# Pooling's joining gate as a stage of seven products, and the last addition of each attention result on GpSimd

## The chip, the core and the metric

The kernel runs on one core of one Trainium2 chip. The metric is the device time of one execution in microseconds, here the median of three runs. A core has TensorE (PE in the profile; PEld are its weight loads), VectorE (DVE), ScalarE (ACT), GpSimd (POOL) and SyncE (SP), which only issues DMAs here. Each engine works through its own list of instructions in order and waits on semaphores for the others.

## The reference, cut to what matters

One decoder block with two parallel branches, on 1024 positions of 1024 channels, in float32:

```python
proj = h @ w_in                       # h: the normalised, modulated input
q, k, v, z_a, u, z_b, m_a, m_b = jnp.split(proj, offs, axis=-1)   # 8 x 1024 columns
attn = stick_breaking_attention(to_heads(q), to_heads(k), to_heads(v))   # 16 heads of 64
p_a = (attn * jax.nn.silu(z_a)) @ w_branch_a
pooled = multiscale_causal_pool(u, pool_w, pool_scale)
p_b = (pooled * jax.nn.silu(z_b)) @ w_branch_b
merged = jax.nn.sigmoid(m_a) * p_a + jax.nn.sigmoid(m_b) * p_b
out = merged @ w_out
return x + gate[:, None, :] * out     # then a final RMS norm
```

The two joining gates are sigmoid(m_a) for attention and sigmoid(m_b) for pooling. In stick-breaking attention a weight is the sigmoid of its own logit times the product of (1 - sigmoid) of all keys between it and the query; the kernel forms that product with a scan along the keys.

## The kernel before

Every matrix is split into a high and a low part, and a product of two matrices is three passes: high by high, high by low, low by high. The input h is kept transposed in `hT`, both parts, 8 blocks of 128 channels by 1024 positions. A column tile is 128 columns of `w_in`; its product with h is 8 blocks x 3 passes for each half of the positions, so 2 x 24 matmuls of 128x128 by 512.

**Stages, in order.** First the modulation, the normalisation and `u` (tiles `ua`, `u`). Then the values, by `seven` (line 565), which multiplies two matrices of 1024x1024, each seen as 2x2 quarters, with seven products of quarters instead of eight (p1, p5, p6, p7, p4, p3, p2; each 2 halves x 4 columns of blocks x 6 matmuls = 48). The sums of quarters of h are made once beforehand (`make_t`, tiles `ht`); those of the weights are made on the way by VectorE, and `copied` and `added` (ScalarE, VectorE) join the products. `values` then splits each result and stores it to DRAM (`v_d`). Then pooling's own gate and projection (`wzb`), and the branch's matrix, again by `seven` (`bp`). The eight banks of PSUM go by four tags of two banks; `any_bank` takes them in turn, and `seven` is told which pair of tags its first chain takes.

**The attention** takes the heads in 8 pairs. For a pair there are three column tiles, keys, queries and gate `za` (`CK`, `CQ`, `CZA`), and in between stand the column tiles of the two joining gates (`CMA`, `CMB`), whose sigmoids go to DRAM. All these tiles are filler: `projections` (line 824) yields after each block of 3 matmuls, a quantum, and `step` (line 1008) weaves so many quanta between the attention's own instructions. `GATES` says how many gate tiles stand in each pair, `QUANTA` how many quanta a pair uses up (70); 37 and 25 quanta go ahead of the first pair, and what is left (18) comes after the last.

A pair has eight units (head h, quarter t of the queries), in `HT_ORDER`. For a unit, `z_items` (line 888) makes logits row block by row block: two matmuls into a bank `z`, two sigmoids on ScalarE (`om` = 1 - sigmoid, `be` = sigmoid), masks on the diagonal block by two selects on GpSimd (line 912), the scan of `om` on VectorE (line 914) and the multiplication of `be` by it. This is done three units ahead. `turn` (line 919) transposes weights chunk by chunk on TensorE into a bank `wt` (two banks), which ScalarE copies (high part) and VectorE subtracts (low part, line 934); two chunks are turned ahead of `product`, so the transposes of the chunk after next wait for a chunk's subtraction. `finish` (line 950) takes the unit's result, which lies in PSUM as three parts: a copy (line 958), two additions on VectorE (line 960), and once both heads are there, the multiplication by `za` on GpSimd and the store to DRAM (lines 963 and 964). A row of logits has up to 1024 keys for t = 0 and as few as 128 for t = 3. The junction of two pairs is where the t = 0 rows of the next pair (1024 and 896 keys) are scanned while its first unit asks for its four chunks.

The weights of each column tile are loaded by SyncE, copied by ScalarE and subtracted by GpSimd (line 116). SyncE's queue also holds the moves of keys and queries between partitions (line 785) and the stores of results. Matmuls, transposes and some others stand in the order of the program; the rest is ordered by the scheduler.

**The final stage** multiplies the gated attention by `w_branch_a` (`pa`), joins the branches with the two gates, read back from DRAM (`sa_d`, `sb_d`), and multiplies by `w_out` (`o`).

Of the kernel before, what the change touches and what calls it, by code (L numbers as in the profile page):

```python
# [21 lines left out]
QUANTA = (70,) * 8  # L22

GATES = (0, 1, 2, 1, 2, 1, 1, 2)
# [27 lines left out]
def block_kernel(ctx, tc, a, out):  # L52
# [17 lines left out]
    turns = [cycle(("av", "tr", "pj", "z")), cycle(("pj", "z", "av", "tr"))]  # L70
# [63 lines left out]
    gates = [c + j for j in range(KB) for c in (CMA, CMB)]  # L134
# [430 lines left out]
    def seven(nm, sums, load, b_of, a_moves, ta, tb, final):  # L565
# [36 lines left out]
        for name in ("p1", "p5", "p6", "p7", "p4", "p3", "p2"):  # L602
# [15 lines left out]
            for j in range(4):  # L618
# [4 lines left out]
                elif name == "p7":  # L623
                    final(1, 1, j, added(copied("s3", 4, j, ps[j]), chain["b"][j]))
                elif name == "p4":
                    final(1, 0, j, ps[j] if a_moves else copied("s3", 4, j + 4, ps[j]))
                elif name == "p3":
                    final(0, 1, j, added(keep["s2", j], ps[j]))
                elif name == "p2":
                    final(0, 0, j, added(keep["s1", j], ps[j]))  # L630

    with pool("vp") as vp:
# [34 lines left out]

        with pool("vs", side="right") as vs:
# [3 lines left out]

            def h_parts(name, q):
                if name in ("p1", "p2", "p3"):
                    k, n = dict(p1=(0, 0), p2=(1, 0), p3=(1, 1))[name]
                    return lambda m, e: hT[:, m, 4 * k + 2 * q + e, 512 * n:512 * n + 512]
                return b_op(k2(tq[("p5", "p6", "p7", "p4").index(name)], q), vs, 2, f"v{name}b{q}")
# [12 lines left out]
            seven("v", vs, load_v_w, h_parts, True, ("av", "tr"), ("pj", "z"), values)  # L690

    turns.pop(0)
# [61 lines left out]
    seven("b", sums, load_b_w, g_parts, False, ("pj", "z"), ("av", "tr"), branch)  # L754
# [5 lines left out]
    with pool("at") as at:  # L760
# [63 lines left out]
        def projections():  # L824

            todo = []
            gates = [(c + j, j, d_) for j in range(KB) for c, d_ in ((CMA, sa_d), (CMB, sb_d))]
# [13 lines left out]
            for i, (ct, p, use) in enumerate(todo):  # L841
# [6 lines left out]
                if gate:  # L848
                    out_ = sigmoid_out(at, 3, use[p], f"m{ct}")
# [100 lines left out]
        def finish(u):  # L950
# [4 lines left out]
            if h == 0:  # L955
                both[t] = at.tile([P, 256], F32, tag="tp", bufs=3, name=f"tp{p}_{t}")
            tp = both[t]
            act.copy(tp[r], av[64:128, 0])
            for i in range(2):
                v.tensor_add(tp[r], av[0:64, i], tp[r])  # L960
            if h == 1:
                sl = slice(t * 256, t * 256 + 256)
                gp.tensor_mul(tp, tp, pair[p]["za"][:, sl])
# [228 lines left out]
```

## Time and profile before

| what | value |
|---|---|
| median of three runs | 1191.57 us (1191.53 to 1192.69) |
| the profiled execution | 1194.0 us, its span 1192.3 us |
| TensorE busy | 1179.2 us (99%) |
| VectorE, ScalarE, GpSimd busy | 826.6, 542.3, 255.1 us |
| values (`vp`) | from 128.3 to 204.5 us |
| pooling's gate (`wzb`), branch (`bp`) | to 291.5, to 368.9 us |
| attention with its filler | to 1011.1 us |
| one pair in the middle | 73.1 us |

A row of the groups reads: line, engine, operation, output<-inputs by the program's names, shapes, count, busy time and mean length of one in ns, then the engine's idle time just before them and who ended it. A row of the timeline reads: start, length, engine, line, operation, tiles, shapes, count, and in brackets the idle time ahead with its releaser. A matmul's length is longer than its share of TensorE, since matmuls are pipelined; the distance from start to start counts. Line numbers are those of the kernel before.

### The profile page before, as it was taken

The numbers are of one execution on the slowest core, as the hardware profiler recorded it, in microseconds if no ns is written. First come the engines' busy times: TensorE is split into PE (matmuls) and PEld (weight loads), VectorE is DVE, ScalarE is ACT, GpSimd is POOL, SyncE is SP. The second block draws the span as 40 slices with busy tenths as digits, with TensorE's granted clock in tenths as the row PEclk, the third lists the DMA queues.
The fourth block names the chain that finished last, engine by engine and source line by source line (L and its number), as shares of the span: only waits on it lengthen the run. The fifth ranks groups of instructions, "written<-read, shape, count | busy, mean of one in ns | idle before, by whom it ended". The sixth has DMA issues, their size and how long they took to land.

```text
span 1192.3 us, 15804 instructions
## 1 busy us (share of the span) xinstructions
PE 1179.2 (99%) x5650; PEld 984.6 (83%) x5650; DVE 826.6 (69%) x1093; ACT 542.3 (45%) x1016; POOL 255.1 (21%) x384
## 2 busy tenths in 40 slices
PE   8999999999999999999999999999999999999997
PEld 7888888888888788888888888888888888888886
DVE  5767466698762577877778687786877853885643
ACT  5561354322541555556556565555555643232111
POOL 1000000000003233244333344333434431000001
PEclk9999999999999999999999999999999999999999
DMA  9652329653457331422415224152321224974612
GB/s 349 259 187 98 131 91 318 229 192 89 142 175 237 92 98 46 136 84 89 106 47 137 85 85 100 56 137 76 113 78 58 71 102 177 346 267 160 228 54 88
DMA packets 73312, 167.26 MB, mean 140 GB/s; under 512 B 9233, under 2 KB 22673, under 8 KB 71058
## 3 DMA queue, kind: packets, MB, share of 16 engines
q1 hardware_dynamic: 65026, 151.38, 39.2%
q10 hardware_dynamic: 8208, 14.88, 3.4%
q8 instruction: 44, 0.72, 0.3%
q14 instruction: 34, 0.28, 0.1%
HBM read 115.89 MB, written 33.56 MB: 125 GB/s over the span
## 4 chain that ended last, share of the span: by engine, by line
PE 82%; DVE 7%; DMA 5%; issue 4%; POOL 1%; ACT 1%; SPq 1%; POOLq 0%; ACTq 0%; DVEq 0%
PE p L101 33%; PE pa L101 7%; PE o L101 6%; PE vp L101 6%; PE z L101 5%; PE av L101 5%; PE wt L101 5%; PE u L101 5%; PE bp L101 4%; PE ua L101 3%; DMA u<-u_d 2%; PE wm L101 1%; DVE om L914 1%; DMA kh<-kh 1%; DVE gb L716 1%
## 5 line engine op out<-in xcount | busy, mean ns | idle before, releaser
L101 PE MATMUL p<-hT,w 128*128 128x512 f32 x1920 | 479.9, 391 | 0.0
L101 PEld LDWEIGHTS p<-hT,w 128*128 128x128 f32 x1920 | 355.2, 188 | 73.9 <-DVE klo L101 0.2
L914 DVE TENSOR_TENSOR_SCAN om<-om 128x512 f32<-128x512 f32 (+7 forms) x128 | 191.2, 1494 | 85.0 <-ACT om L907 51.9
L116 POOL TENSOR_TENSOR w<-w_raw,w 128x1024 fp32r<-128x1024 f32 x39 | 97.2, 2491 | 414.7 <-ACT w L121 409.7
L907 ACT ACTIVATE om<-z 128x512 f32<-128x512 f32 (+2 forms) x192 | 94.6, 493 | 157.1 <-PE z L101 134.6
L934 DVE TENSOR_TENSOR wt<-wt,wt 128x512 fp32r<-128x512 f32 (+1 forms) x160 | 99.4, 621 | 39.4 <-ACT wt L933 38.7
L912 POOL TENSOR_SCALAR_AFFINE_SELECT om<-om 128x128 f32<-128x128 f32 x128 | 72.7, 568 | 205.2 <-ACT om L907 201.8
L933 ACT CAST wt<-wt 128x512 fp32r<-128x512 f32 (+1 forms) x160 | 88.0, 550 | 49.4 <-PE wt L101 49.0
L101 PE MATMUL av<-wt,vv 128*128 128x512 f32 x320 | 106.3, 413 | 0.0
L101 DVE TENSOR_TENSOR be<-be,om 128x511 f32<-128x511 f32 (+7 forms) x128 | 101.1, 794 | 2.0 <-POOL be L912 0.7
L908 ACT ACTIVATE be<-z 128x512 f32<-128x512 f32 (+2 forms) x192 | 94.0, 490 | 0.0
L101 PE MATMUL wt<-ident,be 128*128 128x128 f32 x576 | 89.8, 273 | 1.8 <-DVE wt L934 1.8
L101 PE MATMUL pa<-ga,wa 128*128 128x512 f32 x384 | 89.6, 389 | 0.1
L101 PE MATMUL o<-wo,mhl 128*128 128x512 f32 (+1 forms) x408 | 89.6, 377 | 0.0
L101 PE MATMUL wzb<-hT,wzb 128*128 128x512 f32 x384 | 87.2, 389 | 0.0
L101 PEld LDWEIGHTS o<-wo,mhl 128*128 128x128 f32 x408 | 73.5, 188 | 14.1
L101 PEld LDWEIGHTS pa<-ga,wa 128*128 128x128 f32 x384 | 72.0, 188 | 15.4 <-DVE wa L116 0.5
L101 PEld LDWEIGHTS wzb<-hT,wzb 128*128 128x128 f32 x384 | 72.1, 188 | 14.9
L101 PEld LDWEIGHTS wt<-ident,be 128*128 128x128 f32 x576 | 69.8, 140 | 15.0 <-DVE wt L934 2.5
L101 PE MATMUL z<-kl,q 128*128 128x512 f32 (+2 forms) x192 | 65.5, 341 | 0.0
L101 PE MATMUL z<-kh,q 128*128 128x512 f32 (+2 forms) x192 | 64.0, 334 | 1.1 <-DMA q<-qlo 1.1
L101 PE MATMUL u<-hT,wg 128*128 128x512 f32 x240 | 55.5, 391 | 0.0
(217 smaller groups left out, 1482.0 us busy)
## 6 DMA issues: line engine op xcount, KB each, us to landing
w_raw<-in_w_in SPq DMA_DIRECT2D x40, 512.0 KB, 3.5
v_d<-vo SPq DMA_DIRECT2D x16, 512.0 KB, 4.1
vv<-v_d SPq DMA_DIRECT2D x8, 1024.0 KB, 5.6
wa_raw<-in_w_branch_a SPq DMA_DIRECT2D x16, 512.0 KB, 4.3
wa<-in_w_mod SPq DMA_DIRECT2D x7, 1024.0 KB, 7.5
kh<-kh SPq DMA_DIRECT2D x48, 128.0 KB, 2.3
va<-in_w_v SPq DMA_DIRECT2D x10, 512.0 KB, 3.6
ba<-in_w_branch_b SPq DMA_DIRECT2D x10, 512.0 KB, 4.2
```

The costliest lines, as they stand in the source:

```text
L101: ins = op(*args, **kw)
L116: lo_eng.tensor_tensor(lo, src, hi.bitcast(F32), op=ALU.subtract)
L716: v.scalar_tensor_tensor(z, dhls[j][:, sh * 512:sh * 512 + 512], psc_v[:, j:j + 1], z, ALU.mult, ALU.mult)
L907: act.activation(om[:, b0:b0 + n], zp[:, :n], AF.Sigmoid, scale=-0.125)
L908: act.activation(be[:, b0:b0 + n], zp[:, :n], AF.Sigmoid, scale=0.125)
L912: gp.affine_select(out=tl[:, :P], in_=tl[:, :P], pattern=[[1, P]], compare_op=ALU.is_gt, fill=fill, base=0, channel_multiplier=-1)
L914: v.tensor_tensor_scan(om[:, :W], om[:, :W], om[:, :W], 1.0, ALU.mult, ALU.min)
L933: act.copy(wt[:, 0, :off], pt[:, :off])
L934: v.tensor_sub(wt[:, 1, :off], pt[:, :off], wt[:, 0, :off].bitcast(F32))
```

## The change

Three things are changed together.

**Pooling's joining gate** (`CMB`) leaves the filler and becomes a third use of `seven`, directly behind the values. It reads the same sums of h (`h_parts` is made a function of the pool and the name). `gate_b` takes the sigmoid of each result on ScalarE (of p4's straight from PSUM, of the others from the joined copy) and stores it by SyncE. The weights `w_mb` come in the layout of `w_v`. `seven` gets a parameter `direct`, which says that p4's result is used where it lies in PSUM; the values had that before, and the branch doesn't get it. The tags of banks are exchanged for the new stage and the branch.

**The filler** then holds attention's gate only: 8 gate tiles instead of 16, one each in every other pair and four at the end, and a pair uses up 55 quanta instead of 70. Ten quanta are left after the last pair.

**In `finish`** ScalarE copies two of the three parts (`tl`, `tp`), VectorE adds the third to one of them, and GpSimd adds the two when both heads are there, just ahead of its multiplication.

```diff
-QUANTA = (70,) * 8
-GATES = (0, 1, 2, 1, 2, 1, 1, 2)
+QUANTA = (55,) * 8
+GATES = (0, 1, 0, 1, 0, 1, 0, 1)
...
-    gates = [c + j for j in range(KB) for c in (CMA, CMB)]
+    gates = [CMA + j for j in range(KB)]
...
-                    final(1, 0, j, ps[j] if a_moves else copied("s3", 4, j + 4, ps[j]))
+                    final(1, 0, j, ps[j] if direct else copied("s3", 4, j + 4, ps[j]))
...
+        with pool("ms", side="right") as ms:
+            def load_m_w(t, m, k, q):
+                nc.sync.dma_start(t.rearrange("p k c -> p (k c)"), a["w_mb"][m, 2 * k + q])
+            def gate_b(m, n, j, src):
+                t = ms.tile([P, 512], F32, tag="go", bufs=3, name=f"sb{4 * m + j}_{n}")
+                act.activation(t, src, AF.Sigmoid)
+                nc.sync.dma_start(sb_d[4 * m + j][:, 512 * n:512 * n + 512], t)
+            seven("m", ms, load_m_w, h_parts("m", ms), False, ("pj", "z"), ("av", "tr"), gate_b, True)
...
-    seven("b", sums, load_b_w, g_parts, False, ("pj", "z"), ("av", "tr"), branch)
+    seven("b", sums, load_b_w, g_parts, False, ("av", "tr"), ("pj", "z"), branch, False)
...
-                both[t] = at.tile([P, 256], F32, tag="tp", bufs=3, name=f"tp{p}_{t}")
-            tp = both[t]
-            act.copy(tp[r], av[64:128, 0])
-            for i in range(2):
-                v.tensor_add(tp[r], av[0:64, i], tp[r])
+                both[t] = [at.tile([P, 256], F32, tag=tag, bufs=3, name=f"{tag}{p}_{t}") for tag in ("tp", "tq")]
+            tp, tl = both[t]
+            act.copy(tl[r], av[64:128, 0])
+            act.copy(tp[r], av[0:64, 0])
+            v.tensor_add(tp[r], av[0:64, 1], tp[r])
             if h == 1:
                 sl = slice(t * 256, t * 256 + 256)
+                gp.tensor_add(tp, tp, tl)
                 gp.tensor_mul(tp, tp, pair[p]["za"][:, sl])
```

Three places show what moves. On GpSimd, at the junction of the second and third pairs, stood before (`om`, `be`: the selects, by head, row block; `w_13`: a weights' low part; `tp_1`: the result of t = 1):

```order
L912 AFFINE_SELECT om_0_5_4626<-om_0_5_4626 128x128
L912 AFFINE_SELECT be_0_5_4627<-be_0_5_4627 128x128
L116 TENSOR_TENSOR w_13_4663<-w_13_raw,w_13_4663 128x1024
L963 TENSOR_TENSOR tp_1_4469<-tp_1_4469,za_3626 128x256
L912 AFFINE_SELECT om_1_0_4671<-om_1_0_4671 128x128
L912 AFFINE_SELECT be_1_0_4672<-be_1_0_4672 128x128
```

and at the same junction of GpSimd's list stands now:

```order
L926 AFFINE_SELECT om_0_5_5086<-om_0_5_5086 128x128
L926 AFFINE_SELECT be_0_5_5087<-be_0_5_5087 128x128
L977 TENSOR_TENSOR tp_1_4942<-tp_1_4942,tq_1_4943 128x256
L978 TENSOR_TENSOR tp_1_4942<-tp_1_4942,za_4248 128x256
L926 AFFINE_SELECT om_1_0_5123<-om_1_0_5123 128x128
L926 AFFINE_SELECT be_1_0_5124<-be_1_0_5124 128x128
```

The added addition (L977) stands ahead of the select of the 1024-key row; the weights' low part, whose tile falls elsewhere now, does not. Of the seven junctions it stands directly ahead of that select at one now (the sixth) and at one before (this one).

On TensorE, behind the same junction, stood before (`av`: the products with the values; `p`: filler; `wt`: transposes; `z`: logits):

```order
L101 MATMUL av_0_0_4767<-wt_0_0_1_4716,vv_4504 128x512 x2
L101 MATMUL p_1_4744<-hT,w_12_4501 128x512 x6
L101 MATMUL wt_0_2_2_4805<-ident,be_0_4_4574 128x128 x2
L101 MATMUL wt_0_2_2_4805<-ident,be_0_5_4627 128x128
L101 MATMUL av_0_0_4767<-wt_0_0_2_4756,vv_4504 128x512 x2
L101 MATMUL p_1_4744<-hT,w_12_4501 128x512 x6
L101 MATMUL z_1_5_0_4823<-kh_3796,q_2_3968 128x384
```

and there stands now:

```order
L101 MATMUL av_0_0_5214<-wt_0_0_1_5166,vv_4895 128x512 x2
L101 MATMUL p_1_5186<-hT,w_10_4892 128x512 x6
L101 MATMUL wt_0_2_2_5249<-ident,be_0_4_5032 128x128 x2
L101 MATMUL wt_0_2_2_5249<-ident,be_0_5_5087 128x128
L101 MATMUL av_0_0_5214<-wt_0_0_2_5210,vv_4895 128x512 x2
L101 MATMUL p_1_5186<-hT,w_10_4892 128x512 x3
L101 MATMUL z_1_5_0_5264<-kh_4428,q_2_4669 128x384
```

The attention's own rows are the same; the filler between them is thinner. From the logits of the 1024-key row (`z_1_0_1`) to the transposes `wt_0_2_3` it is 39 matmuls before and 30 now.

On SyncE, at the end of the values, stood before (`v_d`: stores of values; `wzb_raw`: weights of the next stage; `u`: the next stage's input):

```order
L685 DMA v_d<-vo_0_1628 128x4x256
L685 DMA v_d<-vo_0_1633 128x4x256
L129 DMA wzb_raw<-in_w_in 128x1024
L685 DMA v_d<-vo_0_1638 128x4x256
L685 DMA v_d<-vo_0_1643 128x4x256
L703 DMA gbias<-in_b_gate 128x8
L526 DMA u_1662<-u_d 128x1024
```

and there stands now (`ma`: quarters of the new stage's weights):

```order
L687 DMA v_d<-vo_0_1628 128x4x256
L687 DMA v_d<-vo_0_1633 128x4x256
L697 DMA ma_1_1764<-in_w_mb 128x1024
L687 DMA v_d<-vo_0_1638 128x4x256
L687 DMA v_d<-vo_0_1643 128x4x256
L697 DMA ma_0_1728<-in_w_mb 128x1024
L697 DMA ma11s_1731<-in_w_mb 128x1024
L697 DMA ma_1_1766<-in_w_mb 128x1024
```

The stores of values stand where they stood. The new stage's first quarters come between them, and the quarters that its second product adds (`ma_0_1728`, `ma11s_1731` and the next) come behind the last store. In ScalarE's list at the end of the attention, the first weights of the final stage (`wa_0`) are now cast ahead of the last result read back (`ga_7`), and were cast behind it.

More of the change, by code (lines that the diff above doesn't have):

```diff
@@ L68, in bank @@
         return psp.tile([P, 512], F32, tag=tag, bufs=BANKS[tag], name=name)
-    turns = [cycle(("av", "tr", "pj", "z")), cycle(("pj", "z", "av", "tr"))]
+    turns = [cycle(("av", "tr", "pj", "z"))]
     def any_bank(name):
@@ L563, in added, with seven @@
         return t
-    def seven(nm, sums, load, b_of, a_moves, ta, tb, final):
+    def seven(nm, sums, load, b_of, a_moves, ta, tb, final, direct):
         s2k = sums.tile([P, 4, 512], F32, name=nm + "s2k")
@@ L666, in block_kernel, with h_parts, of @@
         early.close()
+        def h_parts(nm, pl):
+            def of(name, q):
+                if name in ("p1", "p2", "p3"):
+                    k, n = dict(p1=(0, 0), p2=(1, 0), p3=(1, 1))[name]
+                    return lambda m, e: hT[:, m, 4 * k + 2 * q + e, 512 * n:512 * n + 512]
+                return b_op(k2(tq[("p5", "p6", "p7", "p4").index(name)], q), pl, 2, f"{nm}{name}b{q}")
+            return of
         with pool("vs", side="right") as vs:
@@ L671, in load_v_w @@
                 nc.sync.dma_start(t.rearrange("p k c -> p (k c)"), a["w_v"][m, 2 * k + q])
[L673 to L677, printed above, removed]
             def values(m, n, j, src):
@@ L688, in values @@
                 )
-            seven("v", vs, load_v_w, h_parts, True, ("av", "tr"), ("pj", "z"), values)
-    turns.pop(0)
+            seven("v", vs, load_v_w, h_parts("v", vs), True, ("av", "tr"), ("pj", "z"), values, True)
+        with pool("ms", side="right") as ms:
[6 more added lines that the diff above has]
+            seven("m", ms, load_m_w, h_parts("m", ms), False, ("pj", "z"), ("av", "tr"), gate_b, True)
+    turns[0] = cycle(("av", "tr", "pj", "z"))
     diffs = ExitStack()
@@ L826, in projections @@
             todo = []
-            gates = [(c + j, j, d_) for j in range(KB) for c, d_ in ((CMA, sa_d), (CMB, sb_d))]
+            gates = [(CMA + j, j, sa_d) for j in range(KB)]
             for p in range(NP):
@@ L848, in projections @@
                 if gate:
-                    out_ = sigmoid_out(at, 3, use[p], f"m{ct}")
+                    out_ = sigmoid_out(at, 2, use[p], f"m{ct}")
                 for sh in range(2):
@@ L1159 @@
     w_v = np.asarray(w_in)[0][:, 2 * D:3 * D].reshape(4, 2, P, 2, 512).transpose(3, 0, 2, 1, 4)
+    w_mb = np.asarray(w_in)[0][:, CMB * P:CMB * P + D].reshape(4, 2, P, 2, 512).transpose(3, 0, 2, 1, 4)
     w_ut = np.asarray(w_in)[0][:, CU * P:CU * P + D].reshape(2, 512, 4, 2, P).transpose(2, 0, 4, 3, 1)
@@ L1178 @@
         "w_v": np.ascontiguousarray(w_v).reshape(2, 4, P, D),
+        "w_mb": np.ascontiguousarray(w_mb).reshape(2, 4, P, D),
         "pool_w": np.ascontiguousarray(np.asarray(pool_w)[0]),
```

## The prediction

> **What bounds the kernel now.** I read the page first, then the list of waits, then the timeline of TensorE alone, then the table of busy time by stage, and last the timeline of one junction between two pairs of heads.
>
> The page's first part and TensorE's own waits:
>
> ```profile
> PE 1179.2 (99%) x5650; PEld 984.6 (83%) x5650; DVE 826.6 (69%) x1093; ACT 542.3 (45%) x1016; POOL 255.1 (21%) x384
> ...
> PE wt L101 <- DVE wt L934: 1.8, 4, 0.5
> ...
> PE z L101 <- DMA q<-qlo: 1.1, 1, 1.1
> ```
>
> TensorE is busy 99% of the span and waits for other engines 3 us in the whole middle of the kernel. A busy TensorE can still hide waits, so the timeline of its groups decides (start, length, group, count):
>
> ```profile
> 128.32 11.04 PE L101 MATMUL vp<-vp1a,hT 128*128 128x512 f32 x48
> 139.20 11.04 PE L101 MATMUL vp<-vp5a,vp5b 128*128 128x512 f32 x48
> ...
> 204.48 87.20 PE L101 MATMUL wzb<-hT,wzb 128*128 128x512 f32 x384
> 291.52 11.17 PE L101 MATMUL bp<-p1b,bp1a 128*128 128x512 f32 x48
> ...
> 313.51 11.55 PE L101 MATMUL bp<-p6b,bp6a 128*128 128x512 f32 x48
> 324.90 11.15 PE L101 MATMUL bp<-p7b,bp7a 128*128 128x512 f32 x48
> ```
>
> From start to start, the values' seven products take 204.48 - 128.32 = 76.16 us for 336 matmuls, and the next stage 291.52 - 204.48 = 87.04 us for 384: 0.2267 us each in both, so nothing waits there. One product of the branch stage (its sixth) takes 324.90 - 313.51 = 11.39 us where 48 x 0.2267 = 10.88: about 0.4 us lost. So the time falls by 0.2267 us for each matmul taken away, until another engine is late. How near the others are, by stage (values; one turn of the loop over pairs):
>
> ```profile
> core 0: us, PE busy (x) PEld busy (x) DVE busy (x) ACT busy (x) POOL busy (x), PEclk, DMA share, GB/s
> 128.30:204.50 76.20, 76.20 (x338) 63.10 (x337) 49.35 (x53) 36.27 (x48) 0.00 (x0) 1.00 0.58 188
> 563.50:636.60 73.10, 73.10 (x373) 61.66 (x372) 57.22 (x76) 41.14 (x89) 25.26 (x40) 1.00 0.35 94
> ```
>
> A pair takes 73.1 us with TensorE at work in all of it; VectorE is busy for 57.22 of them (78%), and all clocks are at 1.00.
>
> **The change: matmuls.** Pooling's joining gate is 8 column tiles of 2 x 24 matmuls, 384, all of them filler in the attention; as seven products it is 7 x 48 = 336. The difference is 48 x 0.2267 = **10.9 us less**. This is the only gain. It takes 15 quanta of 3 matmuls from each of eight pairs: 45 x 0.2267 = 10.2 us, 73.1 becomes 62.9.
>
> **The new stage.** It has the matmuls of the values' stage, whose VectorE and ScalarE work (49.35 and 36.27 of 76.20 us) lay wholly beside TensorE. In place of 16 copies and 16 subtractions it has 16 sigmoids; I cost that at nothing, the cover being TensorE's 76.2 us. What is new is its entry: SyncE issues the weights of its second product behind the last stores of values. The end of the values, on SyncE, and the prices of what follows a load:
>
> ```profile
> 207.72 2.22 SPq L685 DMA_DIRECT2D v_d<-vo  x2
> ...
> va<-in_w_v SPq DMA_DIRECT2D x10, 512.0 KB, 3.6
> ...
> u<-u_d SPq DMA_DIRECT2D x8, 512.0 KB, 5.2
> ...
> L576 DVE TENSOR_TENSOR va<-va,va 128x1024 f32<-128x1024 f32 x2 | 2.4, 1218 | 0.0
> ...
> L548 ACT CAST vp5a<-va 128x1024 fp32r<-128x1024 f32 x2 | 2.1, 1051 | 0.0
> ```
>
> The stores are issued until 209.94, which is 5.5 us after the values' last matmul (204.48). Issue 0.35 (estimated from such rows) and landing 3.6 make 9.4; the addition 1.22 and the cast 1.05 make 11.7. The second product is due at 10.88: **0.9 us** lost, my value, since a load of the same kind and size takes 3.6. The ends: 0 if the load is not held up, and 2.9 if it lands in 5.2 us (2.5) and the sixth product also loses its 0.4.
>
> **The attention.** VectorE loses 64 additions, ScalarE gains 64 copies, GpSimd gains 32 additions, which I price as the multiplication of the same shape:
>
> ```profile
> L960 DVE TENSOR_TENSOR tp<-av,tp 64x256 f32<-64x256 f32 x128 | 52.7, 412 | 2.6
> ...
> L958 ACT COPY tp<-av 64x256 f32<-64x256 f32 x64 | 23.5, 369 | 1.5
> ...
> L963 POOL TENSOR_TENSOR tp<-tp,za 128x256 f32<-128x256 f32 x32 | 27.3, 854 | 66.2 <-DVE tp L960 64.1 <-PE p L101 2.1
> ```
>
> Per pair that is 8 x 0.41 = 3.3 us off VectorE, 8 x 0.37 = 3.0 on ScalarE and 4 x 0.85 = 3.4 on GpSimd. VectorE: 57.2 - 3.3 = 53.9 of 62.9 us, 86%. ScalarE: 44 of 62.9, 70%. Neither is full on average; the average is not what decides. The tight place is the junction, where the longest rows (1024 and 896 keys) of the next pair are scanned while the first result of that pair asks for four chunks. One junction (TensorE, VectorE and GpSimd):
>
> ```profile
> 556.56 2.40 POOL L116 TENSOR_TENSOR w<-w_raw,w 128x1024 fp32r<-128x1024 f32 x1 [1.90 <-ACT w L121]
> ...
> 557.69 1.52 PE L101 MATMUL p<-hT,w 128*128 128x512 f32 x6
> 557.89 0.60 ACT L907 ACTIVATE om<-z 128x512 f32<-128x512 f32 x1 [0.43 <-PE z L101]
> ...
> 558.92 0.75 POOL L963 TENSOR_TENSOR tp<-tp,za 128x256 f32<-128x256 f32 x1
> ...
> 559.95 2.35 DVE L914 TENSOR_TENSOR_SCAN om<-om 128x1024 f32<-128x1024 f32 x1 [2.84 <-POOL om L912]
> ...
> 560.38 2.01 POOL L912 TENSOR_SCALAR_AFFINE_SELECT om<-om 128x128 f32<-128x128 f32 x1 [0.22 <-ACT om L907]
> ...
> 570.39 0.66 DVE L934 TENSOR_TENSOR wt<-wt,wt 128x512 fp32r<-128x512 f32 x1
> ...
> 571.53 0.60 PE L101 MATMUL wt<-ident,be 128*128 128x128 f32 x4
> ```
>
> The logits of the 1024-key row end at 557.69. The scan starts only at 559.95: its select stood on GpSimd behind the weights' low part (2.40) and the multiplication (0.75). From there VectorE works without a pause to the chunk's subtraction, which ends at 571.05, and the transposes of the chunk after next, which need that PSUM bank, start at 571.53: 0.5 us of slack. Now the change. TensorE's way from 557.69 to 571.53 is 13.84 us with 39 filler matmuls; 30 are left, so 13.84 - 9 x 0.2267 = 11.8. VectorE's way is 11.1, less one of its two additions, 10.7. So there is room for a lag of 1.1 us between the logits and the scan. If GpSimd is free, the lag is what ScalarE's second sigmoid needs, 558.49 - 557.69 = 0.8: no wait. If the weights' low part stands ahead again, the lag is 2.26 and the added 0.75: 3.0, a wait of 1.9 us. I take **0.7 us**, nearer to the free end: in the changed order the low part stands directly ahead of this select at one junction of seven (it was one before, too, the one shown), and the added addition at all seven. Seven junctions: 4.9 us; ends 0 and 13.3.
>
> Other ways at nothing. The stores of results now wait for one more GpSimd instruction on SyncE's queue, and behind them stand the moves of keys and queries:
>
> ```profile
> 388.35 4.45 DMA q<-q
> 392.81 2.33 DMA q<-qlo
> ```
>
> That chain takes 6.8 us. The tightest case is pair 6: the first half of its query tile ends at quantum 360 and its first logits come at 371, 33 matmuls or 7.5 us and the attention's work between; it holds, and were it not so it would cost a microsecond or two at pairs 2, 4 and 6. The filler behind the last result shrinks from 18 to 10 quanta and from 81 matmuls to 51:
>
> ```profile
> 992.70 18.55 PE L101 MATMUL p<-hT,w 128*128 128x512 f32 x81
> 1011.09 4.24 PE L101 MATMUL pa<-ga,wa 128*128 128x512 f32 x18
> ...
> 1002.57 0.62 ACT L873 CAST ga<-gr 128x512 fp32r<-128x512 f32 x1 [7.01 <-DMA gr<-ga_d]
> ...
> 1004.66 1.23 DVE L116 TENSOR_TENSOR wa<-wa_raw,wa 128x1024 fp32r<-128x1024 f32 x1 [0.74 <-ACT wa L121]
> ```
>
> The cover falls by 30 x 0.2267 = 6.8 us. The first weights of the final stage were ready at 1005.89, 5.2 us early; they would now be 1.6 late, but the new order casts them ahead of the result that ScalarE waited 7.01 us for. Nothing, then; 1.6 if that fails.
>
> **The sum** against the profiled execution: -10.9 + 0.9 + 4.9 = -5.1 us, a span of 1187.2 instead of 1192.3. That execution took 1194.0 and the median of three runs is 1191.57; taking the same from the median gives **1186.5 us**.
>
> **The rivals.** *Everything stays covered*: the scans start 0.8 us after their logits at every junction. For it: VectorE falls idle before the junction scan. Against it: only 0.5 us of slack is left now. It gives 1191.6 - 10.9 + 0.9 = 1181.6, or 1180.7 without the entry's loss.
>
> *The junctions eat the gain*: a wait of (10.9 - 0.9) / 7 = 1.4 us each brings back 1191.6. It needs a lag of 2.5, which the row above nearly has (2.26).
>
> *Slower: GpSimd's additions hold up VectorE.* While the scan from 559.95 to 562.30 ran, GpSimd's select took 2.01 us and ended at 562.39. It goes the other way too:
>
> ```profile
> 706.96 2.61 POOL L116 TENSOR_TENSOR w<-w_raw,w 128x1024 fp32r<-128x1024 f32 x1 [2.25 <-ACT w L121]
> ...
> 708.99 1.67 DVE L101 TENSOR_TENSOR be<-be,om 128x1023 f32<-128x1023 f32 x1
> ...
> 562.81 1.21 DVE L101 TENSOR_TENSOR be<-be,om 128x1023 f32<-128x1023 f32 x1
> ```
>
> The multiplication begun at 708.99, before GpSimd was done at 709.57, took 0.46 us more than its like. If every added addition holds the scans so, 4 x 0.85 = 3.4 us a pair undoes the relief of 3.3, and the two additions that fall into a junction add 1.7 to its 0.7: 7 x 2.4 = 16.8, and 16.8 + 0.9 - 10.9 = +6.8, 1198.4 us. It decides from 1.4 us a junction. Against it: the addition waits for VectorE's own result, so it often starts when VectorE has just come free. The Trainium skill, page "SBUF — State Buffer", section "Who interferes with whom", states this as a rule: a VectorE instruction with two SBUF inputs and a GpSimd instruction that reads SBUF exclude each other for a whole instruction. The trace agrees (the 2.01 us select and the 1.67 us multiplication); by that rule alone, applied to every addition, the sum would be this rival's.
>
> *The stage doesn't run as seven full products* because sigmoids in ScalarE's order delay its casts: 36 of 76 us leave room for that, so I give it no chance of its own.
>
> **Chances.** All covered 0.20; forecast 0.42 (waits of 0.3 to 1.1 us a junction, 1183.7 to 1189.3); gain eaten 0.20; slower 0.18. A measurement of this kernel tells about 0.2%, 2.4 us, from no change. Faster by more than that: the first two, 0.62; the same 0.20; slower 0.18. The range reaches from the covered case to most of the slower one, 1181.0 to 1196.0.
>
> **What would show it.** The gate's seven products should take 76.2 us from start to start and up to 1 us more, the loss between its first and second product. A pair should take 62.9 us and 0.7 more, with waits of TensorE's transposes for the chunks' subtractions just behind the 1024-key scan, and with the scan released by GpSimd's select. If the pairs take 62.9 flat, the first rival holds. If they take over 64.3, it is one of the other two: with two-input VectorE instructions lengthened beside the added additions it is the slower one. Waits of logits for the moves of queries, or of the final stage for its weights, would make steps wrong that I priced at nothing.

## The result, and the profile after

The changed kernel takes 1207.62 us (median of 4 runs, 1205.8 to 1209.85), the kernel before 1191.89 (1191.53 to 1192.69). The ratio is 1.0132, 95% interval 1.0114 to 1.015: 1.3% slower, where 0.4% faster was forecast. The profiled execution has a span of 1205.7 us, 13.4 more than the profiled one before. The medians lie 15.7 apart, since that execution before was itself slower (1194.0) than all four that were timed; the accounts below explain the 13.4.

The first part of the page and TensorE's own waits, of the changed kernel:

```profile
PE 1172.3 (97%) x5602; PEld 975.0 (81%) x5602; DVE 844.2 (70%) x1071; ACT 586.0 (49%) x1106; POOL 287.9 (24%) x408
...
PE wt L101 <- DVE wt L948: 12.7, 14, 1.8
PE mp L101 <- ACT mp5a L548: 3.8, 1, 3.8
PE mp L101 <- DVE mp6b L555: 2.0, 1, 2.0
PE wt L101 <- DVE be L101: 1.9, 4, 0.6
...
PE z L101 <- DMA q<-qlo: 1.6, 1, 1.6
```

The 48 matmuls are gone (5650 to 5602), but TensorE waits in two places where it did not: twice in the new stage (5.8 us), and at 18 transposes of the attention (14.6 us; 1.8 before). The timeline of TensorE, changed kernel (start, length, group, count, and in brackets the idle time ahead of the group and what ended it):

```profile
204.65 11.04 PE L101 MATMUL mp<-hT,mp1a 128*128 128x512 f32 x48
219.52 12.79 PE L101 MATMUL mp<-mp5b,mp5a 128*128 128x512 f32 x48 [3.83 <-ACT mp5a L548]
...
235.23 10.27 PE L101 MATMUL mp<-mp6b,mp6a 128*128 128x512 f32 x44 [2.02 <-DVE mp6b L555]
245.33 11.04 PE L101 MATMUL mp<-mp7b,mp7a 128*128 128x512 f32 x48
...
288.85 87.20 PE L101 MATMUL wzb<-hT,wzb 128*128 128x512 f32 x384
...
452.81 25.53 PE L101 MATMUL p<-hT,w 128*128 128x512 f32 x111
...
574.26 0.66 PE L101 MATMUL wt<-ident,be 128*128 128x128 f32 x4 [1.63 <-DVE wt L948]
587.96 0.66 PE L101 MATMUL wt<-ident,be 128*128 128x128 f32 x4 [1.79 <-DVE wt L948]
641.74 0.66 PE L101 MATMUL wt<-ident,be 128*128 128x128 f32 x4 [1.62 <-DVE wt L948]
704.80 0.52 PE L101 MATMUL wt<-ident,be 128*128 128x128 f32 x3 [0.92 <-DVE wt L948]
708.10 0.65 PE L101 MATMUL wt<-ident,be 128*128 128x128 f32 x4 [1.27 <-DVE wt L948]
...
1024.03 6.28 PE L101 MATMUL pa<-ga,wa 128*128 128x512 f32 x27
```

And where the attention begins in the kernel before (it ends at 1011.09, the row is in the prediction):

```profile
368.85 25.35 PE L101 MATMUL p<-hT,w 128*128 128x512 f32 x111
```

The new stage takes 288.85 - 204.65 = 84.2 us where 76.2 is the matmuls' own time: **8.0 lost**. The attention takes 1024.03 - 452.81 = 571.2; before it took 642.2, and without its 384 gate matmuls (87.05 us) that is 555.2: **16.0 lost**. So the span went by 84.2 - 87.05 + 16.0 = +13.2, of the 13.4 measured. All of the question is in these two numbers. The waits that the timeline shows in the attention sum to 16.3 us (2.8 before); so of the 16.0 us 13.5 are added waits, and 2.5 are not listed as waits of any group. A pair takes 65.6 us (six pairs, from the 1024-key scan at 561.7 to the one at 955.6), more than the 64.3 at which the prediction gave up its forecast.

In the stage, four things show. Its products run in the order p1, p5, p6, p7, p4, p3, p2; p5 is the second product here and the fifth in some of the expectations, p6 is the sixth. Timeline of SyncE, ScalarE and VectorE, then the table of busy time by stretch (its last four columns: GpSimd, granted clock, DMA share, GB/s), changed kernel:

```profile
209.21 1.25 SPq L697 DMA_DIRECT2D ma<-in_w_mb  x1
210.51 0.74 SPq L697 DMA_DIRECT2D ma11s<-in_w_mb  x1
...
212.83 0.59 ACT L598 COPY ms<-mp 128x512 f32<-128x512 f32 x1 [4.79 <-PE mp L101]
...
214.40 2.36 DVE L555 TENSOR_TENSOR mp5b<-ht,mp5b 128x1024 fp32r<-128x1024 f32 x2 [5.63 <-ACT mp5b L554]
...
217.16 1.23 DVE L576 TENSOR_TENSOR ma<-ma,ma 128x1024 f32<-128x1024 f32 x1 [0.40 <-DMA ma<-in_w_mb]
```

```profile
195.00:200.00 5.00, 5.00 (x24) 4.14 (x23) 2.69 (x4) 2.19 (x4) 0.00 (x0) 1.00 1.06 333
...
210.00:215.00 5.00, 5.00 (x24) 4.14 (x23) 0.60 (x1) 2.17 (x3) 0.00 (x0) 1.00 1.03 379
...
219.60:223.00 3.40, 3.40 (x9) 2.71 (x10) 2.33 (x3) 0.00 (x0) 0.00 (x0) 0.57 0.89 286
223.00:226.00 3.00, 3.00 (x13) 2.41 (x12) 1.67 (x3) 1.05 (x1) 0.00 (x0) 0.92 0.89 356
```

The load whose addition opens the second product is issued from 209.21, as forecast, but its addition runs at 217.16. The page's landing times count from the start of the issue; by that count this load took 7.9 us, not 3.6. Two loads that the kernel before issues among the values' stores were nearly as slow. The two loads with their landing, changed kernel, then kernel before:

```profile
L697 SPq DMA_DIRECT2D ma<-in_w_mb x1: 1247/1247/1247, 209.2 to 209.2; - x1
...
DMA to landing us min/median/max: 7.9/7.9/7.9
```

```profile
L671 SPq DMA_DIRECT2D va<-in_w_v x2: 345/346/346, 180.3 to 185.3; - x2
...
DMA to landing us min/median/max: 6.3/6.4/6.6
```

While the load is under way the DMA engines are full (a share of 1.03; a transfer is booked where it starts, so a share can pass 1). Beside it ScalarE is late: the casts of the second product's other factor (`mp5b`) stand behind a copy that waits 4.79 us for the first product, and VectorE's two subtractions, which wait for these casts, end only at 216.76, 0.4 us before the addition. And behind the 3.83 us wait the granted clock is 0.57: the second product runs for 12.79 us instead of 11.04, though only its start had to wait.

At a junction of the attention, VectorE and GpSimd, changed kernel:

```profile
695.24 2.35 DVE L928 TENSOR_TENSOR_SCAN om<-om 128x1024 f32<-128x1024 f32 x1 [1.92 <-POOL om L926]
...
699.79 2.40 POOL L116 TENSOR_TENSOR w<-w_raw,w 128x1024 fp32r<-128x1024 f32 x1 [1.86 <-ACT w L121]
700.39 3.68 DVE L928 TENSOR_TENSOR_SCAN om<-om 128x896 f32<-128x896 f32 x1
702.14 2.45 POOL L977 TENSOR_TENSOR tp<-tp,tq 128x256 f32<-128x256 f32 x1
704.00 0.66 DVE L948 TENSOR_TENSOR wt<-wt,wt 128x512 fp32r<-128x512 f32 x1
```

GpSimd's subtraction for the weights' low part ends at 702.19; the 896-key scan, begun beside it, takes 3.68 us. The added addition in turn lasts until the scan is over (702.14 to 704.59; 0.74 at other places). Behind the scan stands the subtraction (704.00) for which the transposes at 704.80 wait. Two suspects, then: the old instruction and the new one.

### The profile page after: what moved, and what is told of

Its sections match the earlier page's. It is cut to its first block, busy times and chain, and to the rows that moved or that the text cites. A ratio compares the mean times of both kernels' runs of the same rounds, so it can differ in the third digit from the quotient of the medians.

```text
span 1205.7 us, 15897 instructions
## 1 busy us (share of the span) xinstructions
PE 1172.3 (97%) x5602; PEld 975.0 (81%) x5602; DVE 844.2 (70%) x1071; ACT 586.0 (49%) x1106; POOL 287.9 (24%) x408
## 4 chain that ended last, share of the span: by engine, by line
PE 79%; DVE 9%; DMA 4%; issue 4%; POOL 2%; ACT 2%; SPq 0%; POOLq 0%; DVEq 0%; ACTq 0%
PE p L101 20%; PE wzb L101 7%; PE pa L101 7%; PE bp L101 6%; PE o L101 6%; PE vp L101 6%; PE mp L101 5%; PE u L101 5%; PE z L101 4%; PE av L101 4%; PE wt L101 4%; DVE om L928 3%; PE ua L101 3%; DVE be L101 2%; PE wm L101 1%
## 5 line engine op out<-in xcount | busy, mean ns | idle before, releaser
L101 PE MATMUL p<-hT,w 128*128 128x512 f32 x1536 | 392.6, 392 | 0.0
L101 PEld LDWEIGHTS p<-hT,w 128*128 128x128 f32 x1536 | 283.1, 188 | 58.0 <-DVE klo L101 0.3
L928 DVE TENSOR_TENSOR_SCAN om<-om 128x512 f32<-128x512 f32 (+7 forms) x128 | 185.6, 1451 | 68.1 <-POOL om L926 36.4
L116 POOL TENSOR_TENSOR w<-w_raw,w 128x1024 fp32r<-128x1024 f32 x31 | 78.4, 2528 | 453.4 <-ACT w L121 448.3
L921 ACT ACTIVATE om<-z 128x512 f32<-128x512 f32 (+2 forms) x192 | 94.8, 494 | 117.3 <-PE z L101 78.4
L926 POOL TENSOR_SCALAR_AFFINE_SELECT om<-om 128x128 f32<-128x128 f32 x128 | 78.0, 610 | 166.8 <-ACT om L921 147.9
L101 DVE TENSOR_TENSOR be<-be,om 128x511 f32<-128x511 f32 (+7 forms) x128 | 107.6, 845 | 1.7 <-POOL be L926 0.5
L101 PE MATMUL wt<-ident,be 128*128 128x128 f32 x576 | 90.7, 274 | 14.6 <-DVE wt L948 12.7
```

The lines of the kernel that those rows point to most:

```text
L101: ins = op(*args, **kw)
L116: lo_eng.tensor_tensor(lo, src, hi.bitcast(F32), op=ALU.subtract)
L921: act.activation(om[:, b0:b0 + n], zp[:, :n], AF.Sigmoid, scale=-0.125)
L926: gp.affine_select(out=tl[:, :P], in_=tl[:, :P], pattern=[[1, P]], compare_op=ALU.is_gt, fill=fill, base=0, channel_multiplier=-1)
L928: v.tensor_tensor_scan(om[:, :W], om[:, :W], om[:, :W], 1.0, ALU.mult, ALU.min)
```

## Experiments on the attention

Theory G: the addition on GpSimd makes the junction late (the mechanism of the rival that was slower). Theory F: the cover is thinner by 15 quanta a pair, and that is enough. Below, "waits" are the sum of TensorE's waits in the attention by the timeline.

**The old finish in the changed kernel.**

```diff
-            act.copy(tl[r], av[64:128, 0])
-            act.copy(tp[r], av[0:64, 0])
-            v.tensor_add(tp[r], av[0:64, 1], tp[r])
+            act.copy(tp[r], av[64:128, 0])
+            for i in range(2):
+                v.tensor_add(tp[r], av[0:64, i], tp[r])
...
-                gp.tensor_add(tp, tp, tl)
```

> The changed kernel with the attention results finished as before: one copy on ScalarE, both additions on VectorE, none on GpSimd. The gate stage and the thinner filler stay. Theory G (GpSimd's addition and VectorE's scans hold each other up at the junctions): TensorE's gaps in the attention fall from 16 us to 2 or less, time 1192 to 1194. Theory F (15 quanta less filler a pair leave too little work ahead of the transposes, whatever the finish): 12 to 18 us of gaps stay, time 1204 to 1210. If it takes both: 5 to 10 us of gaps, 1197 to 1202.

Measured: 1206.68 us, ratio to before 1.0124 (1.0104 to 1.0144), waits 16.9 us. Theory G falls. TensorE's waits in this run:

```profile
PE wt L101 <- DVE wt L948: 8.0, 8, 1.8
PE wt L101 <- POOL tp L977: 5.2, 4, 3.0
```

The second row names GpSimd's multiplication of the results, but at each of its four waits VectorE's subtraction had ended only 0.1 us earlier, so that subtraction is what is late there as well.

**The new finish alone, in the kernel before.** The edit is the one above the other way round, with the gates' buffers cut from three to two.

> The kernel before with the new finish alone: 70 quanta a pair, both gates as filler, the last addition on GpSimd (the gates' output buffers go from three to two, as in the change, to make room). Theory G: gaps of 12 to 17 us in the attention, time 1204 to 1209. Theory F: at most 2 us, time 1190 to 1194. If it takes both: under 5 us, 1191 to 1197.

Measured: 1193.79 us, ratio 1.0012 (1.0003 to 1.0022), waits 2.8 us. By itself the new finish costs 1.4 us (0.4 to 2.6) by the medians and adds no waits; it isn't the cause.

**The kernel before with thinner cover.**

```diff
-QUANTA = (70,) * 8
+QUANTA = (55,) * 8
-GATES = (0, 1, 2, 1, 2, 1, 1, 2)
+GATES = (0, 1, 0, 1, 0, 1, 0, 1)
```

> The kernel before with nothing changed but how its filler is dealt out: 55 quanta a pair in place of 70 and the gates' tiles in the places of the changed kernel; the filler that is left over runs behind the last pair. No gate stage, the old finish, the same work in all. If the thinner cover alone brings the stalls of the attention: gaps of 13 to 18 us in place of 2.8, time 1203 to 1209. If they need the gate stage or the new finish as well: under 6 us, 1191 to 1196.

Measured: 1208.01 us, ratio 1.0135 (1.0121 to 1.0149), waits 13.1 us. Same work, same finish, no new stage, and the attention takes 654.9 us, 12.7 more than in the kernel before: most of the changed kernel's 16.0. That the two kernels' times agree as well is chance, since the changed one has the stage's loss and the saved matmuls besides. TensorE's waits in this run:

```profile
PE wt L101 <- DVE wt L934: 8.7, 9, 1.8
PE wt L101 <- POOL tp L963: 2.3, 3, 1.1
```

So taking 15 quanta from each pair (with the gate tiles placed as the change places them) is what brings most of the stalls. It doesn't yet say what is late.

**Without the weights' low part on GpSimd** (that part of the product is left out; the high part is multiplied in its place).

```diff
+        hl = wts.tile([P, 2, KB, P], F32R, tag="whl", bufs=2, name=name)
+        act.copy(hl[:, 0], raw)
+        return hl[:, 0], hl[:, 0]
```

> The changed kernel without the low part of the weights of the attention's filler (the high part stands in its place in the matmuls, so that part of the result is left out): GpSimd has no subtraction of 2.4 to 2.5 us any more, all else is as it was. Theory P (at the junction the 896-column scan is stretched from 2.0 to 3.4 to 4.3 us by that subtraction, and the transposes behind it wait): gaps in the attention fall from 16.3 us to 4 to 9. Theory D (VectorE has more to do in the junction's steps than they last, the stretching only adds a little): 11 to 15 stay. Time 1207.5 less the difference.

Measured: 1194.35 us, waits 4.6 us. The attention takes 556.9 us, 1.7 above the 555.2 of no loss, though the stage ahead of it still lost its part. The scan of 896 keys and the subtraction, in the groups of instructions by shape, of the kernel before, of the changed one and of this one (line, engine, operation, count, busy us, mean ns):

```profile
L116 POOL TENSOR_TENSOR w<-w_raw,w 128x1024 fp32r<-128x1024 f32 x39 | 97.2, 2491 | 414.7 <-ACT w L121 409.7 <-DMA kh<-kh 5.0
...
L914 DVE TENSOR_TENSOR_SCAN om<-om 128x896 f32<-128x896 f32 x16 | 36.0, 2248 | 1.1 <-issue 0.5 <-ACT om L907 0.3
```

```profile
L116 POOL TENSOR_TENSOR w<-w_raw,w 128x1024 fp32r<-128x1024 f32 x31 | 78.4, 2528 | 453.4 <-ACT w L121 448.3 <-DMA kh<-kh 5.1
...
L928 DVE TENSOR_TENSOR_SCAN om<-om 128x896 f32<-128x896 f32 x16 | 36.3, 2271 | 1.2 <-issue 0.5 <-ACT om L921 0.5
```

```profile
L934 DVE TENSOR_TENSOR_SCAN om<-om 128x896 f32<-128x896 f32 x16 | 32.3, 2020 | 1.2 <-issue 0.5 <-ACT om L927 0.5
```

The scan is held up as much in the kernel before (2248 ns) as in the changed one (2271), and not at all without the subtraction (2020). The delay is old; the thicker cover hid it. The means hide how few are hit: two of the 16 scans take over 3.3 us in the kernel before and two in the changed one, of which only one, the one shown, is at a junction. The subtraction falls on other rows too. GpSimd and VectorE ahead of the longest wait of the attention, the 1.79 us at 587.96, changed kernel:

```profile
583.59 2.39 POOL L116 TENSOR_TENSOR w<-w_raw,w 128x1024 fp32r<-128x1024 f32 x1 [1.33 <-ACT w L121]
...
583.89 3.43 DVE L928 TENSOR_TENSOR_SCAN om<-om 128x640 f32<-128x640 f32 x1 [2.03 <-ACT om L921]
```

A scan of 640 keys takes 1.49 us on average in the run without the subtraction. With thin cover and no subtraction 4.6 us of waits are left, with thick cover and the subtraction 2.8: the large loss takes both.

**Without the selection on om** (the diagonal blocks of the first factor stay unmasked).

```diff
-                        for tl, fill in ((om, 1.0), (be, 0.0)):
+                        for tl, fill in ((be, 0.0),):
```

> The changed kernel without the mask of the first factor (GpSimd's selection on om is left out, so the diagonal blocks are not masked there; the selection on be stays). The scan then waits for ScalarE alone. Theory L (the scan starts late because GpSimd's addition and multiplication stand ahead of the selection: VectorE idle 1.92 us at 693.3 to 695.24): gaps fall from 16.3 us to 5 to 10. Theories P and D: 12 to 17 stay.

Measured: 1206.56 us, waits 14.8. The six profiles whose code for the attention is the same (the changed kernel's, and the first five of the next section) have 14.7 to 16.5, so this is no effect that one profile could show, and theory L falls. The lag between logits and scan, on which the prediction's term was built, is worth 1.5 us of the 16.3 at most.

**The subtraction in four pieces, and on VectorE.**

```diff
-    lo_eng.tensor_tensor(lo, src, hi.bitcast(F32), op=ALU.subtract)
+    for i in range(n):
+        lo_eng.tensor_tensor(lo[:, s], src[:, s], hi[:, s].bitcast(F32), op=ALU.subtract)
```

Here n is 4 on GpSimd, and s a quarter.

> The changed kernel with GpSimd's subtraction for the low part of the filler's weights cut into four instructions of a quarter each. Theory P (one long instruction of GpSimd holds the scan up for its whole length): a scan is held up by a quarter, 0.6 us, at a time; the 896-column scan falls from a mean of 2271 ns towards 2100, gaps in the attention from 16.3 us to 8 to 13, time 1199 to 1204. If only the sum of GpSimd's work counts: no change, 1205 to 1209.

Measured: 1201.97 us, ratio 1.0085 (1.0068 to 1.0102), waits 10.9. GpSimd's sum for it rises from 78.4 to 106.8 us and the loss still falls: the length of one hold counts, and not the sum alone.

```diff
-        return load_w(a["w_in"][tiles[i]], name, act, v if i == MASKED else gp)
+        return load_w(a["w_in"][tiles[i]], name, act, v)
```

> The changed kernel with the low part of the filler's weights subtracted on VectorE (1.22 us each by the branch stages' rows) in place of GpSimd (2.53 us): no long instruction is left on GpSimd, VectorE gets 31 x 1.22 = 38 us more. Theory P (what counts is the scan held up by GpSimd, up to 2.4 us a time at the junction): gaps fall from 16.3 us to 8 to 14, as 1.2 us takes the place of up to 2.4. Theory D (VectorE's sum of work counts): gaps rise to 20 to 35 us, time 1211 to 1226.

Measured: 1202.27 us, waits 12.0. Here VectorE has 39.4 us more to do (32 x 1.23 by its row) and TensorE waits 4.3 us less than in the changed kernel. VectorE's sum of work, then, is not what decides (theory D predicted 20 to 35).

**The quanta dealt unevenly over a pair.**

```diff
-SHARE = (7,) * 8
+SHARE = (7, 7, 5, 6, 5, 8, 7, 10)
```

> The changed kernel with its 55 quanta a pair dealt out in the steps of a pair as 7,7,5,6,5,8,7,10 in place of 7 each: more filler where VectorE has the two widest pairs of scans (sixth and last step), less where it has little. Theory D: gaps in the attention fall from 16.3 us to 3 to 8, time 1194 to 1200. Theory P: the subtraction still falls on the scan of the junction, gaps 12 to 18, time 1203 to 1209.

Measured: 1203.07 us, ratio 1.0087 (1.007 to 1.0103), waits 10.5: between the two theories' figures. The waits behind the last step go, others come early in a pair (1.25 us at 668.57, 1.30 at 911.71). Cover moved to one place is missing at another.

## Experiments on the stage's entry

Theory C: ScalarE's order (the casts of the second product behind a copy that waits 4.8 us). Theory S or Q: SyncE's queue. Theory W: the load on the DMA engines. One caution for all of them: the stage took 83.9 to 87.4 us in seven profiles whose code for it is the same, so a difference of 2 us in one profile shows little.

```diff
             if name == "p1" and nm == "m":
+                early = [b_of("p5", q) for q in range(2)]
```

> The changed kernel; in the gate stage the two casts of the second product's activations stand ahead of the copies of the first product's results on ScalarE. Theory C (ScalarE waits 4.8 us in the first copy with these casts behind it, and VectorE's subtractions and the weights' addition come late by that): the stage falls from 84.2 us to 77 to 79. Theory S (the weights of the second product land late behind the stores of the values): 83 to 84.5, the addition still runs at 217. If either alone suffices to be late: 82 to 84 here, and only both cures together bring it to 77.

Measured: stage 86.8 us (1210.0). VectorE then stands idle 5.44 us for the load, until 217.66: with the casts on time, the load alone makes the addition as late. Theory C alone falls.

```diff
-                nc.sync.dma_start(
+                (gp if (m, n) == (0, 0) else nc.sync).dma_start(
```

> The changed kernel; the last four stores of the values are issued by GpSimd, so that SyncE's queue goes on with the loads of the gate stage without waiting for them. Theory S: the loads land 3 to 6 us earlier, the stage falls from 84.2 us to 77 to 79. Theory C: it stays at 82 to 84.5, as the casts of the second product still stand behind the first copy on ScalarE. If either alone suffices to be late: 82 to 84.

Measured: stage 82.0 us (1203.08). Some 2 us off, not the 5 to 7 of theory S. The load, issued at 207.64, lands after 6.7 us, at 214.3, but the addition runs at 216.35, behind a subtraction that waits for ScalarE until 215.21: the late casts alone suffice, too.

Both edits together:

> The changed kernel with both cures of the gate stage's entry: casts of the second product ahead of the copies on ScalarE, last four stores of the values issued by GpSimd. With the casts alone the stage took 86.8 us and the first addition of weights waited for its load (VectorE idle until 217.66); with the stores alone 82.0, and the addition ran at 216.35 behind the late subtractions. Theory B (loads and casts are late side by side, the later one decides): stage 78 to 80 us, second product's wait at most 1.5 us. Theory Q (the loads of the second product also stand behind a load of its own second half, which waits for a buffer until 207): stage 80 to 82, as the loads are issued at 208 with the stores out of the way.

Measured: stage 84.0 us (1206.36). A miss for theory B, and for theory Q. The second product's waits fell to 1.62 and 1.00 us, the sixth's grew to 2.76, with the clock at 0.64 to 0.75 behind it: the late loads of the second half took over.

```diff
-        for name in ("p1", "p5", "p6", "p7", "p4", "p3", "p2"):
+        for name in ("p1", "p2", "p5", "p6", "p7", "p4", "p3") if nm == "m" else (...):
```

> The changed kernel with the gate stage's products in the order 1, 2, 5, 6, 7, 4, 3: the second product issued is one whose weights need no addition, and the fifth product's loads, additions and casts get 10.9 us more. The two cures at ScalarE and SyncE together had left the stage at 84.0 us (the fifth product's wait fell from 3.8 to 2.6 us in two pieces, but the sixth's rose from 2.0 to 2.8, and both products ran longer). Theory E (all of the stage's 8 us are the late chain of load, addition, cast and subtraction of the fifth product's weights, on through its second half and the sixth product): the stage takes 76.2 to 78. Theory V (VectorE's work in the first half of the stage is too much for the time in any order): 81 to 85.

Measured: stage 82.2 us (1202.92), and inconclusive: product p5 now waits 2.94 us for PSUM banks that p2 has just filled, a wait of the edit's own making, and runs 13.97 us, with the clock at 0.50 for the first 6.

```diff
-            t = (wts if first else sums).tile(...)
+            t = (wts if first else sums if nm == "b" else vp).tile(...)
```

With the early casts as well:

> The changed kernel with the gate stage's second buffer of weights in the pool that both stages share (so that the fifth product's loads need not wait until the values' tiles are free; SyncE's order then has two of its loads ahead of the last eight stores of the values' other half), and the fifth product's casts ahead of the copies on ScalarE. Theory E (the late chain of load, addition, cast and subtraction makes all of the stage's 8 us): the stage takes 76.2 to 78.5. Theory V (VectorE's work in the first half of the stage is too much in any order): 81 to 85.

Measured: stage 79.1 us (1204.69; here the stretch ahead of the stage was 2.2 us longer). That is between the two theories. Two loads issued ahead of the stores take 5 of the 8 us away; the waits left, 1.86 and 0.46, leave the clock at 1.00.

```diff
+                w = 16 if m == 0 else 4 * HD
...
-                    v_d[4 * m:4 * m + 4, :, sb].rearrange(...)
+                    v_d[4 * m:4 * m + 4, :, sb, :w].rearrange(...)
```

> The changed kernel with the last eight stores of the values (half of v_d) cut from 512 KB to 32 KB each, and the attention's first four pairs reading the other half's values (so these values are left out of the result). SyncE's order of loads and stores stays; the scheduler puts the fifth product's casts ahead of the copies on ScalarE, which alone had not shortened the stage. Theory W (the loads of the fifth product land late because the DMA engines are busy 93 to 106 per cent of the time from 180 to 215 us with the values' stores): the loads land in 3.5 to 4.5 us in place of 6 to 7.6, the stage takes 77 to 80 us. Theory Q (they are late by their place in SyncE's queue alone): the stage stays at 82 to 87.

Measured: stage 76.6 us (1200.1), as good as without loss. The timeline of TensorE, the first addition on VectorE, and the table by stretch, of this run:

```profile
204.54 11.04 PE L101 MATMUL mp<-hT,mp1a 128*128 128x512 f32 x48
215.63 11.24 PE L101 MATMUL mp<-mp5b,mp5a 128*128 128x512 f32 x48
...
281.11 29.18 PE L101 MATMUL wzb<-hT,wzb 128*128 128x512 f32 x128
```

```profile
213.26 1.23 DVE L576 TENSOR_TENSOR ma<-ma,ma 128x1024 f32<-128x1024 f32 x1 [2.64 <-DMA ma<-in_w_mb]
```

```profile
195.00:200.00 5.00, 5.00 (x23) 4.13 (x22) 3.73 (x6) 2.90 (x4) 0.00 (x0) 1.00 0.54 75
...
205.00:210.00 5.00, 5.00 (x24) 4.14 (x23) 5.00 (x7) 3.78 (x5) 0.00 (x0) 1.00 0.48 63
```

The load that decides stands where it stood in SyncE's queue, behind the last store, yet the first addition runs at 213.26 instead of 217.16. Of these 3.9 us 1.3 come from an earlier issue (207.93 instead of 209.21, the short stores being issued sooner) and 2.6 from landing (5.2 us, against 7.9; 3.5 to 4.5 was expected). So, with the casts early, the values' stores make the entry late in both ways, through the queue and through the engines, and nearly all of the loss goes with them. The attention of this run waits 16.1 us as before: the two losses are separate.

**The cures together.** Shared buffer, early casts, pieces, with the dealing of the run above, or a milder one; the third run adds the stores on GpSimd.

```diff
-SHARE = (7,) * 8
+SHARE = (7, 7, 6, 6, 6, 7, 7, 9)
```

> The changed kernel with the shared buffer, the early casts, the low parts of the weights in four pieces, and the quanta dealt 7,7,5,6,5,8,7,10. If the losses are independent: gate stage 77 (from 84.2), gaps in the attention 5 to 8 (from 16.3; the pieces alone left 10.9 and the dealing alone 10.5), time 1189 to 1193, the same as or a little faster than the kernel before. If the cures of the attention meet in the same stalls: gaps 9 to 11, 1194 to 1197.

> As the run before, with a milder dealing, 7,7,6,6,6,7,7,9 (the dealing 7,7,5,6,5,8,7,10 had brought new waits early in a pair, 1.0 to 1.3 us at 537.5, 668.6 and 911.7, while those of the junction went). Gaps in the attention 4 to 8, time 1188 to 1193; if the cures meet in the same stalls 9 to 11, 1194 to 1197.

> The kernel with the shared buffer, early casts, pieces and the dealing 7,7,6,6,6,7,7,9 (1190.06 us), and the last four stores of the values issued by GpSimd as well. If the 2.9 us that the gate stage still loses are the second half's loads behind these stores on SyncE: stage 77 to 78, time 1188 to 1190. If it is the DMA engines' load by the stores, whoever issues them: stage 79, time 1189.5 to 1191.

Measured: 1196.42 us, ratio 1.004 (1.0027 to 1.0054), for the first dealing; 1190.06, ratio 0.9981 (0.9972 to 0.999), for the milder one; 1190.04, the same ratio, with the stores moved as well, so that last edit does nothing here. The waits are 11.7, 6.5 and 6.1 us, the stage 82.8, 78.9 and 78.8. The first one's profile is of the slowest of its six executions (1200.99 us); its stage is the same code as the second's: its wait happened to last 3.55 us and cost it the clock. TensorE's waits in the second one:

```profile
PE wt L101 <- DVE wt L955: 4.6, 8, 1.5
...
PE mp L101 <- DVE mp5b L559: 1.5, 1, 1.5
```

That is 17.6 us better than the changed kernel and 0.2% better than the kernel before (2.2 us of the 10.9 that the matmuls gave).

## Why the prediction was wrong

- *The matmuls, -10.9 us.* Right: 48 fewer, and where nothing waits a product takes 10.88 us from start to start.
- *The entry, 0.9 us; 8.0 measured.* The issue time was right to a microsecond (209.2). The failed step is "since a load of the same kind and size takes 3.6": that is the median of loads over the whole stage. The loads that matter go out while the stores fill the DMA engines, and the trace of the kernel before has two such loads, with 6.3 and 6.6 us. The step puts the addition at 213.9 (209.94 + 0.35 + 3.6), and it ran at 217.16. A second step failed beside it, "I give it no chance of its own" for casts delayed by ScalarE's order. They were late, not by sigmoids but by a copy that waits 4.79 us, and the two runs with one cure each show that either lateness is enough. Earlier loads and early casts together took 5 of the 8.0 away, short stores and early casts 7.6. Nor did the term hold what follows: the second half's loads go out only when the first half's additions have freed their buffers (218.42, behind the addition that ends at 218.39), and so the sixth product waits too (2.0); and the clock fell behind the long wait, which made the second product 1.75 us longer. The upper end, 2.9, was a landing of 5.2 us and thus no bound. (The term's own sum, 11.7 less 10.88, is 0.8, and its 0.35 for the issue is counted twice, as the landing time includes it; both are small.)
- *The attention, 4.9 us; 16.0 measured.* The failed step is "VectorE's way is 11.1, less one of its two additions, 10.7", with only the lag ahead of the scan left free, and "Seven junctions: 4.9 us", which puts every other place at nothing. VectorE's way wasn't fixed: the prediction took it from one junction, where the low part ended before the scans began. At the junction shown above the subtraction lies beside the 896-key scan and lengthens that way by 1.7 us (3.68 against 2.02). That is one junction of seven; at other places the subtraction falls on other scans and on multiplications. Leaving it out brought the waits from 16.3 to 4.6; the lag itself was worth 1.5 us at most. And a junction has more than one wait (0.92 and 1.27 at that one): by the timeline 9.6 of the 16.3 us stand behind the seven junctions, 1.4 each where 0.7 was forecast, and 6.7 elsewhere, of which 1.6 are the logits' wait named below. What is late at each of the waits was not worked out one by one; at 574.26 and 641.74 it is a select on GpSimd behind the added addition.
- *The slower rival* had the right sign, the right kind of mechanism (two-input VectorE instructions and GpSimd shutting each other out) and, at 16.8 us, nearly the right price for the attention; that is luck, as it was added up from another instruction. It named the wrong instruction: the added addition, which the two runs on the finish clear, in place of the subtraction that was there all along and that the prediction had quoted twice. The runs clear the addition of the loss as a whole, not of each single wait.
- *Priced at nothing.* The sigmoids and the end of the attention cost nothing that shows. The logits' wait for the moves of queries went from 1.1 to 1.6 us.
- *The covers.* The prediction read the cover at one junction of the kernel as it was. That kernel had its junctions covered by 10.2 us a pair of the very matmuls that the change takes away; running that kernel with its filler dealt as thinly showed 12.7 of the 16.0 us in one line.

Left open: what keeps 4 to 6 us of waits in the attention without the subtraction or in the best dealing, the 3.3 us of the attention's loss that thinner cover alone doesn't bring, and why the stage's waits differ between equal profiles. What its scatter consists of the traces show: in all 16 profiles with the stage its time is 76.2 us, its listed waits, and half of the time at the half clock, to 0.8 us; in the seven equal ones the waits are 4.3 to 7.7 us and that time 3.4 or 6.8.

## What to carry to other kernels

Before filler is taken out of a loop, run the old kernel with the filler dealt thinner and nothing else changed: it prices the cover directly. A load's landing time is read in the stretch where it will be issued, with the DMA share of that stretch beside it, not from a median over the program. When an engine shares a port or a lock with the one on the path, list every instruction of it that can fall beside the path, the old ones first.

## What the runs showed of the hardware

**A short stop of TensorE can cost twice.** In the middle of the kernel, over all 19 traces, the granted clock stayed at 1.00 behind every wait of up to 2.27 us. With waits of 2.66 us and more it fell to 0.50, for 3.4 or 6.8 us, in 15 of 16 cases; one of 3.34 us left it at 1.00. (The clock of a stretch in these tables is a mean, so 0.57 holds some full clock.) The table by stretch, of the changed kernel with the old finish, behind a wait of 2.97 us:

```profile
835.80:838.50 2.70, 2.68 (x8) 2.26 (x9) 2.70 (x4) 0.48 (x1) 1.30 (x2) 0.53 0.15 49
838.50:842.00 3.50, 3.50 (x18) 3.01 (x17) 2.64 (x5) 1.72 (x4) 1.28 (x2) 0.88 0.02 5
```

The filler's matmuls start 0.43 us apart there (837.26, 837.68, 838.11) instead of 0.23. The Trainium skill, page "TensorE: Matmul & The Clock Gate", section "What's actually happening", gives half rate after an idle window of about 3.4 us, on a window that runs freely. The half rate agrees; here stops of 2.66 to 3.3 us were enough in all cases but one, and the measurement decides.

**GpSimd and VectorE exclude each other also in the scan.** A scan of 896 keys takes 2.02 us by itself and up to 4.26 beside the 2.4 us subtraction (in the changed kernel with the old finish). It fits the rule of the Trainium skill, page "SBUF — State Buffer", section "Who interferes with whom", that the prediction cites.
